# Two-layer hybrid trunk, one core: the first two projection units multiplied together, and weights loaded in half tiles

## The chip, the cores and the metric

The kernel runs on one core of a Trainium2 chip. The metric is device time of one execution in microseconds (us), the median of several runs. The engines are called as the profile calls them: PE is the matrix engine (PEld its weight loads), DVE the vector engine, ACT the scalar engine, POOL the GpSimd engine, and SP is the queue from which all DMAs of this kernel are issued.

## The reference

A residual trunk of two layers over x (1024 tokens by 1024 features, float32). Layer 0 has a gated DeltaNet head group and a sparse attention head group whose keys are picked by an indexer; layer 1 has stick-breaking attention and the HGRN2 recurrence. Each layer is a mixer and a SwiGLU feed-forward part, each between two RMS norms:

```python
for l in range(DEPTH):
    y = rms_norm(h, norm_g[l, 0])
    y = even_mixer(...) if l % 2 == 0 else odd_mixer(...)     # p = y @ w_in, heads, @ w_out
    h = h + rms_norm(y, norm_g[l, 1])
    y = swiglu(rms_norm(h, norm_g[l, 2]), w_gate[l], w_up[l], w_down[l])
    h = h + rms_norm(y, norm_g[l, 3])
```

Layer 0's `w_in` gives, among others, the 1536 columns q, k, v of the DeltaNet heads and a small group of columns for the indexer's key and the gates.

## The kernel before

**Tiling.** Features lie on the 128 partitions, tokens in two halves of 512 columns. All weights are cut into units of 128 x 1024 values (512 KB), for one feature-major unit the eight 128 x 128 blocks of one 128-column slice of a matrix. `wload` (L228) fetches a unit by one DMA into `wraw` (two buffers) and cuts it into a rounded part and a rest: ACT copies each half of 512 columns to `whi` in a rounded format (`split`, L193), and DVE for the first half, POOL for the second, subtract it from the raw values to give `wlo` (L197). `whi` and `wlo` have four half buffers each, so two units fit. The activations are cut the same way into `yhi` and `ylo` (`y_tile`, L332 and L336). A product is then three passes: `whi` by `yhi` and `whi` by `ylo` (the high passes) and `wlo` by `yhi` (the low pass), 24 matmuls of 512 columns for a feature-major unit (`dense_fm`, L264).

**Order within a unit.** `passes` (L240) takes the eight blocks in two parts of four: four high by high, four high by rest, the same for the other four, then the low pass in the same two parts. With several sums (`dense_tm`, L270, and `outproj`, L410) it goes over all sums in each part.

**The start.** `run` (L1279) calls `consts` (L150), which loads `gg` (norm gains and others) and `cc` (identity, a triangle and ones, 192 KB). `first_norm(0)` (L360) loads the eight 128 x 512 tiles of x for the first token half, cuts each into `yhi` and `ylo` with the norm's gain, and sums the squares (ACT L295 and L298, DVE L299); the inverse root mean square `rd` is applied only behind the matmuls (`norms`, L346, with the matmul with ones at L306, then ACT L308 and L309). `proj_even_a(0)` (L566) multiplies unit `U_KI` first; DVE scales the result with `rd` into `stage` (L579) and four small transposes at L583 take the gate columns from it. Then come the twelve units `U_QKV`, each followed by a scaled copy out of PSUM (`scaled`, L258), a causal convolution of four taps on DVE (L595 and three of L597), a sigmoid on ACT and a product on DVE (L600), and a store (L601). DeltaNet loads these again (L706), and its chunks start from there.

**What sets the order.** Each engine works through its instructions in a fixed order, and so does SP's queue of DMAs. A planner wrote this order beforehand from modelled times: at each moment the ready instruction with the highest priority goes next. What stands under `first()` has a far higher priority than the rest: loads, splits, norms and the work behind a matmul; the matmuls of `passes` do not. PSUM gives the projections three banks (`acc`), one the letter `b` and one `a`, three `w`.

**The end.** The last feed-forward product goes in two column halves (`down_halves`, L488), which load the same four units twice, and `last_residual` (L504) follows each.

Of the kernel before, what the change touches and what calls it, by code (L numbers as in the profile page):

```python
# [13 lines left out]
F32R = mybir.dt.float32r  # L14
# [8 lines left out]
P = 128  # L23
# [4 lines left out]
KD = 8  # L28
# [14 lines left out]
U_QKV, U_KI, U_QI, U_QB, U_KB, U_VB, U_Z = 0, 12, 13, 17, 21, 25, 29  # L43
# [68 lines left out]
class Trunk:  # L112
# [37 lines left out]
    def consts(self):  # L150
        nc, cp = self.nc, self.cp
        nc.scalar.preload_act_table_set("natural_log_exp_and_others")
        self.cc = self.t(cp, [P, C_COLS], "cc")
        c = lambda o: self.cc[:, o:o + P]
        self.ident, self.ut, self.ones = c(C_ID), c(C_U), c(C_ONES)
        self.gg = self.t(cp, [P, G_COLS], "gg")
        with self.first():
            nc.sync.dma_start(self.gg, self.ins["p_cols"])
            nc.sync.dma_start(self.cc, self.ins["c_main"])
        self.k = self.t(self.np_, [P, 8], "kk")  # L160
        nc.vector.memset(self.k[:, 0:1], -0.5)
        nc.vector.memset(self.k[:, 1:2], 1e-6)
        nc.vector.memset(self.k[:, 2:3], -0.5 * math.log(P))
        nc.vector.memset(self.k[:, 3:4], 1.0)
        nc.vector.memset(self.k[:, 4:5], 0.0)
        self.nhalf = self.k[:, 0:1]
        self.eps, self.lnscale, self.one = self.k[:, 1:2], self.k[:, 2:3], self.k[:, 3:4]
# [60 lines left out]
    def wload(self, u):  # L228
        nc = self.nc
        with self.first():  # L230
            raw = self.t(self.wp, [P, 1024], "wraw")
            nc.sync.dma_start(raw, self.ins["w_units"][u])
            w = []
            for c, e in ((slice(0, 512), nc.vector), (slice(512, 1024), nc.gpsimd)):
                w.append(self.split(raw[:, c], *(self.t(self.wp, [P, 512], n, F32R, bufs=4) for n in ("whi", "wlo")), (e,)))
        self.pace()

        return lambda o, n=P: [t[:, o % 512:o % 512 + n] for t in w[o // 512]]

    def passes(self, sums, w, first=True, last=True):  # L240

        mm = self.nc.tensor.matmul
        order = [((0, 0), (0, 1)), ((1, 0),)] if w == 0 else [((0, 0), (1, 0)), ((0, 1),)]
        n = len(sums[0][2]) // 2
        seq = [(g, ps, l[a], r[b]) for pairs in order for part in (slice(0, n), slice(n, None))
               for a, b in pairs for g, ps, terms in sums for l, r in terms[part]]
        begun, end = set(), {g: i for i, (g, *_) in enumerate(seq)}
        for i, (g, ps, l, r) in enumerate(seq):  # L250
            mm(ps, l, r, start=first and g not in begun, stop=last and end[g] == i)  # L251
            begun.add(g)
# [11 lines left out]
    def dense_fm(self, u, y):  # L264
        w = self.wload(u)
        ps = self.acc()
        self.passes([(0, ps, [(w(k * P), y.t[k]) for k in range(KD)])], 0)
        return ps

    def dense_tm(self, u0, y):  # L270

        n = HS // 2
        for c in range(2):
            ps = [self.acc() for _ in range(2)]
            for u in range(2):
                w = self.wload(u0 + 2 * c + u)
                self.passes([(tt // 2, ps[tt // 2][:, tt % 2 * n:tt % 2 * n + n],
                              [([t[:, tt * P:(tt + 1) * P] for t in y.t[4 * u + j]], w(j * n, n))
                               for j in range(4)]) for tt in range(NT)], 1, u == 0, u == 1)
            for i in range(2):  # L280
                yield 2 * i, c * n, ps[i]
# [78 lines left out]
    def first_norm(self, half):  # L360
        with self.first():
            tiles, acc, y = [], None, Y()
            for k in range(KD):
                x = self.part()
                self.nc.sync.dma_start(x, self.ins["x"][k * P:(k + 1) * P, half * HS:(half + 1) * HS])
                if half == 0:
                    self.y_tile(y, k, x, self.ng(0, 0, k))
                else:
                    acc = self.sumsq(acc, k, x)
                tiles.append(x)  # L370
            if half:
                return self.to_y(0, 0, tiles, self.inv_rms(acc))
            self.norms(y, tiles, True)
            return y
# [191 lines left out]
    def proj_even_a(self, half, y):  # L566
        nc = self.nc
        if half == 0:
            self.hist = self.t(self.np_, [P, 12, 3], "hist")
            nc.vector.memset(self.hist, 0.0)  # L570
            self.ab = self.t(self.cp, [P, 8, 16], "ab")
            self.an = self.head_gain(self.cp, "a_norm")
        ps = self.dense_fm(U_KI, y)
        with self.first():
            s = self.t(self.hp, [P, HS], "stage", bufs=2)
            if y.r is None:
                nc.vector.tensor_copy(s[0:80], ps[0:80])
            else:
                nc.vector.tensor_tensor(out=s[0:80], in0=ps[0:80], in1=y.r[0:80], op=OP.mult)  # L579
            nc.sync.dma_start(self.kiT[half], s[0:64])  # L580
            pt = self.acc()
            for tt in range(NT):
                nc.tensor.transpose(pt[:, tt * 16:tt * 16 + 16], s[64:80, tt * P:(tt + 1) * P], self.ident[64:80, 64:80])  # L583
            nc.vector.tensor_copy(self.ab[:, half * 4:half * 4 + 4, :],
                                  pt[:, 0:64].rearrange("p (t c) -> p t c", t=4))
        for ct in range(12):
            ps = self.dense_fm(U_QKV + ct, y)
            with self.first():
                xp = self.t(self.small, [P, HS + 3], "xp")
                nc.vector.tensor_copy(xp[:, 0:3], self.hist[:, ct, :])  # L590
                self.scaled(xp[:, 3:], ps, y, dve=False)
                nc.vector.tensor_copy(self.hist[:, ct, :], xp[:, HS:])
                cw = lambda j: self.gg[:, G_CONV + ct * 4 + j:G_CONV + ct * 4 + j + 1]
                s = self.t(self.hp, [P, HS], "stage", bufs=2)
                nc.vector.tensor_scalar(s, xp[:, 0:HS], cw(0), None, op0=OP.mult)  # L595
                for j in range(1, 4):
                    nc.vector.scalar_tensor_tensor(s, xp[:, j:j + HS], cw(j), s, op0=OP.mult, op1=OP.add)  # L597
                sig = self.t(self.hp, [P, HS], "sq")
                self.sigmoid(sig, s)
                nc.vector.tensor_tensor(out=s, in0=sig, in1=s, op=OP.mult)  # L600
                nc.sync.dma_start(self.qkvT[half][ct * P:(ct + 1) * P], s)  # L601
        self.tm_store(U_Z, y, self.zs[half], gain=self.an)
# [861 lines left out]
```

## Time and profile before

| | us |
|---|---|
| median of three runs | 2910.11 |
| the three runs | 2907.5 to 2910.74 |
| the profiled execution, its own time | 2903.69 |
| its span, first to last instruction | 2901.9 |
| PE busy in it | 2818.6 (97%) |

The profile is of one execution. Its page gives busy times of the engines, the span in slices, and the costliest groups of instructions; the trace behind it can be asked for the instructions in order of time (a timeline, where neighbouring instructions of one kind are merged into one row with their count), for who waited for whom, and for busy time and granted clock in any stretch. Busy PE time counts slow matmuls as fully as fast ones.

### The profile page before, as it was taken

How to read it: one execution, taken by the hardware profiler on the slowest of the kernel's cores; microseconds unless marked ns; L12 is line 12 of the kernel's file. 1: busy time of each engine (PE TensorE's matmuls, PEld its weight loads, DVE VectorE, ACT ScalarE, POOL GpSimd, SP SyncE). 2: the span in 40 equal slices, each digit the busy share in tenths (PEclk: the TensorE clock that was granted, in tenths of full speed). 3: DMA queues.
4: the chain of work that ended last, by engine and by line, in shares of the span. 5: the costliest groups of instructions: out<-in, count | busy, mean ns of one | idle time of the engine just before them, and what ended most of it. 6: DMA issues, size and time to landing. Idle time of an engine off the chain costs nothing. (4 is left out here: it accounts for less than half of the span.)

```text
span 2901.9 us, 41648 instructions
## 1 busy us (share of the span) xinstructions
PE 2818.6 (97%) x14850; PEld 2351.2 (81%) x14850; DVE 1694.5 (58%) x3037; ACT 1574.0 (54%) x2893; POOL 1123.3 (39%) x916
## 2 busy tenths in 40 slices
PE   8999999999999998999999999999999999999997
PEld 6888888878787886978788888889778778788886
DVE  7857973675656557378665235736666544732235
ACT  5545863666657585254664335536666544543333
POOL 3323332344435342255554332325555432333332
PEclk9999999999999999999999999999999999999999
DMA  5433446243333334446333334654323323543233
GB/s 196 136 121 109 144 151 209 91 146 114 103 117 107 104 121 137 139 147 202 111 109 95 100 97 125 231 156 128 98 87 107 98 89 115 167 149 98 95 95 109
DMA packets 200975, 366.63 MB, mean 126 GB/s; under 512 B 16544, under 2 KB 104640, under 8 KB 200768
## 3 DMA queue, kind: packets, MB, share of 16 engines
q1 hardware_dynamic: 200768, 363.97, 39.6%
q8 instruction: 117, 1.92, 0.3%
q14 instruction: 90, 0.74, 0.1%
HBM read 306.23 MB, written 57.67 MB: 125 GB/s over the span
## 5 line engine op out<-in xcount | busy, mean ns | idle before, releaser
L197 POOL TENSOR_TENSOR wlo<-wraw,whi 128x512 fp32r<-128x512 f32 x422 | 589.1, 1396 | 1240.3 <-PE acc L251 497.3
L193 ACT ACTIVATE whi<-wraw 128x512 fp32r<-128x512 f32 x844 | 521.6, 625 | 487.0 <-PE acc L251 431.2
L197 DVE TENSOR_TENSOR wlo<-wraw,whi 128x512 fp32r<-128x512 f32 x422 | 337.9, 801 | 470.7 <-PE acc L251 355.5
L251 PE MATMUL acc<-yhi,whi 128*128 128x512 f32 x2064 | 585.3, 400 | 11.8 <-ACT whi L193 8.0
L251 PE MATMUL acc<-ylo,whi 128*128 128x512 f32 x2064 | 581.9, 398 | 2.2 <-DVE ylo L336 2.2
L251 PE MATMUL acc<-yhi,wlo 128*128 128x512 f32 x2064 | 536.1, 396 | 0.0
L251 PE MATMUL acc<-act,whi 128*128 128x512 f32 (+1 forms) x1984 | 510.6, 393 | 21.3 <-DVE stage L452 5.7
L251 PEld LDWEIGHTS acc<-yhi,whi 128*128 128x128 f32 x2064 | 386.1, 189 | 99.5 <-ACT whi L193 8.0
L251 PEld LDWEIGHTS acc<-ylo,whi 128*128 128x128 f32 x2064 | 386.3, 189 | 88.3 <-issue 6.0
L251 PEld LDWEIGHTS acc<-yhi,wlo 128*128 128x128 f32 x2064 | 383.7, 188 | 84.1 <-issue 6.1
L251 PEld LDWEIGHTS acc<-act,whi 128*128 128x128 f32 x1984 | 363.1, 189 | 109.3 <-issue 11.5
L251 PE MATMUL acc<-act,wlo 128*128 128x512 f32 (+1 forms) x992 | 266.6, 386 | 1.4 <-POOL wlo L197 1.4
L251 PEld LDWEIGHTS acc<-act,wlo 128*128 128x128 f32 x992 | 182.0, 188 | 38.5 <-POOL wlo L197 1.8
L950 ACT ACTIVATE pen<-sc,tk 128x384 bf16<-128x384 f32 (+4 forms) x155 | 155.3, 1002 | 52.2 <-DVE tk L954 46.1
L480 DVE TENSOR_TENSOR part<-acc,part 128x512 f32<-128x512 f32 x152 | 103.8, 685 | 66.2 <-PE acc L251 66.0
L193 ACT ACTIVATE act<-stage 128x512 fp32r<-128x512 f32 x104 | 65.2, 629 | 136.9 <-DVE stage L459 117.0
L197 POOL TENSOR_TENSOR act<-stage,act 128x512 fp32r<-128x512 f32 x88 | 120.2, 1366 | 43.1 <-ACT act L193 41.0
L299 DVE TENSOR_TENSOR ssq<-ssq,sq 128x512 f32<-128x512 f32 (+1 forms) x119 | 98.7, 830 | 27.2 <-ACT sq L298 25.0
L951 DVE TENSOR_SCALAR tk<-tk 128x1 uint32<-128x1 f32 x186 | 39.3, 211 | 125.4 <-ACT pen L950 124.9
L452 DVE TENSOR_TENSOR stage<-acc,stage 128x512 f32<-128x512 f32 x66 | 45.5, 689 | 98.3 <-ACT stage L220 98.2
L251 PE MATMUL acc<-whi,yhi 128*128 128x256 f32 x640 | 100.1, 287 | 1.6 <-DVE stage L552 1.6
L251 PE MATMUL acc<-whi,ylo 128*128 128x256 f32 x640 | 101.3, 287 | 0.0
(461 smaller groups left out, 4038.1 us busy)
## 6 DMA issues: line engine op xcount, KB each, us to landing
wraw<-in_w_units_dram SPq DMA_DIRECT2D x422, 512.0 KB, 3.6
h<-part SPq DMA_DIRECT2D x40, 256.0 KB, 3.9
hld<-h SPq DMA_DIRECT2D x40, 256.0 KB, 4.6
qkvT<-stage SPq DMA_DIRECT2D x24, 256.0 KB, 2.5
kT<-kbT SPq DMA_DIRECT2D x24, 256.0 KB, 3.6
vv<-vb SPq DMA_DIRECT2D x24, 256.0 KB, 3.0
qkv<-qkvT SPq DMA_DIRECT2D x18, 256.0 KB, 3.6
part<-in_x_dram SPq DMA_DIRECT2D x16, 256.0 KB, 6.3
```

Source lines behind the costliest of these rows:

```text
L193: nc.scalar.activation(hi, src, AF.Copy)
L197: e.tensor_tensor(out=lo[:, c], in0=src[:, c], in1=hi[:, c].bitcast(F32), op=OP.subtract)
L251: mm(ps, l, r, start=first and g not in begun, stop=last and end[g] == i)
L299: nc.vector.tensor_tensor(out=acc, in0=acc, in1=sq, op=OP.add)
L452: nc.vector.tensor_tensor(out=s, in0=pg, in1=s, op=OP.mult)
L480: nc.vector.tensor_tensor(out=parts[d], in0=ps, in1=parts[d], op=OP.add)
L950: sc.activation(pen, s, AF.Sign, scale=sg, bias=nb, accum_out=n)
L951: v.tensor_scalar(rej.bitcast(U32), n, th, float(1 << b), op0=OP.is_lt, op1=OP.mult)
```

## The change

Four things change. The first two units of layer 0 (`U_KI` and the first of `U_QKV`), for the first token half only, are loaded together and go through one call of `passes` with eight steps: for each tile k of x the high passes of both units, and after all eight tiles the low pass of one unit and then of the other. Each raw unit comes by two DMAs of 256 KB into four half buffers (the same memory as before), and each half is split from its own buffer. The low pass of `passes` now goes through all the terms of one sum before the next sum, everywhere. The load of `cc` is issued in `first_norm(0)` behind the loads of x.

```diff
@@ consts
         with self.first():
             nc.sync.dma_start(self.gg, self.ins["p_cols"])
-            nc.sync.dma_start(self.cc, self.ins["c_main"])
@@ wload
         with self.first():
-            raw = self.t(self.wp, [P, 1024], "wraw")
-            nc.sync.dma_start(raw, self.ins["w_units"][u])
             w = []
             for c, e in ((slice(0, 512), nc.vector), (slice(512, 1024), nc.gpsimd)):
-                w.append(self.split(raw[:, c], *(self.t(self.wp, [P, 512], n, F32R, bufs=4) for n in ("whi", "wlo")), (e,)))
+                raw = self.t(self.wp, [P, 512], "wraw", bufs=4)
+                nc.sync.dma_start(raw, self.ins["w_units"][u][:, c])
+                w.append(self.split(raw, *(self.t(self.wp, [P, 512], n, F32R, bufs=4) for n in ("whi", "wlo")), (e,)))
         self.pace()
@@ passes
-    def passes(self, sums, w, first=True, last=True):
+    def passes(self, sums, w, first=True, last=True, steps=2):
         mm = self.nc.tensor.matmul
         order = [((0, 0), (0, 1)), ((1, 0),)] if w == 0 else [((0, 0), (1, 0)), ((0, 1),)]
-        n = len(sums[0][2]) // 2
-        seq = [(g, ps, l[a], r[b]) for pairs in order for part in (slice(0, n), slice(n, None))
-               for a, b in pairs for g, ps, terms in sums for l, r in terms[part]]
+        n = len(sums[0][2]) // steps
+        parts = [slice(i * n, (i + 1) * n) for i in range(steps)]
+        high, low = order
+        seq = [(g, ps, l[a], r[b]) for part in parts for a, b in high for g, ps, terms in sums for l, r in terms[part]]
+        seq += [(g, ps, l[a], r[b]) for a, b in low for g, ps, terms in sums for l, r in terms]
@@ behind dense_fm
+    def dense_pair(self, us, y):
+
+        ws, pss = [self.wload(u) for u in us], [self.acc() for _ in us]
+        self.passes([(i, ps, [(w(k * P), y.t[k]) for k in range(KD)]) for i, (w, ps) in enumerate(zip(ws, pss))], 0, steps=KD)
+        return pss
@@ first_norm
                 tiles.append(x)
+            if half == 0:
+                self.nc.sync.dma_start(self.cc, self.ins["c_main"])
@@ proj_even_a
-        ps = self.dense_fm(U_KI, y)
+        ps, first = self.dense_pair((U_KI, U_QKV), y) if half == 0 else (self.dense_fm(U_KI, y), None)
...
         for ct in range(12):
-            ps = self.dense_fm(U_QKV + ct, y)
+            ps = first if half + ct == 0 else self.dense_fm(U_QKV + ct, y)
```

## Rows read from the trace of the kernel before

**Rows 1.** Page, part 1: busy us, share of the span, instructions of each engine.

```profile
PE 2818.6 (97%) x14850; PEld 2351.2 (81%) x14850; DVE 1694.5 (58%) x3037; ACT 1574.0 (54%) x2893; POOL 1123.3 (39%) x916
```

**Rows 2.** Timeline of PE, 0 to 36: start, us, what, [idle before <-releaser].

```profile
8.04 0.80 PE L251 MATMUL acc<-yhi,whi 128*128 128x512 f32 x1 [8.04 <-ACT whi L193]
9.18 0.80 PE L251 MATMUL acc<-yhi,whi 128*128 128x512 f32 x1 [0.34 <-ACT yhi L332]
...
17.19 2.00 PE L251 MATMUL acc<-yhi,wlo 128*128 128x512 f32 x8
20.34 1.13 PE L306 MATMUL b<-ssq,cc 128*128 128x512 f32 x2 [1.15 <-DVE ssq L299]
...
24.57 0.42 PE L583 MATMUL acc<-cc,stage 16*128 16x16 f32 x4
24.91 1.84 PE L251 MATMUL acc<-yhi,whi 128*128 128x512 f32 x4
...
31.25 0.91 PE L858 MATMUL w<-lg,pt 32*128 32x384 f32 x2
...
33.34 1.09 PE L251 MATMUL acc<-yhi,whi 128*128 128x512 f32 x4
```

**Rows 3.** Timeline of ACT, 0 to 36.

```profile
4.51 0.72 ACT L332 ACTIVATE yhi<-part,gg 128x512 fp32r<-128x512 f32 x1 [1.68 <-DMA part<-in_x_dram]
...
7.36 1.15 ACT L193 ACTIVATE whi<-wraw 128x512 fp32r<-128x512 f32 x2 [1.62 <-DMA wraw<-in_w_units_dram]
...
14.17 0.71 ACT L332 ACTIVATE yhi<-part,gg 128x512 fp32r<-128x512 f32 x1
...
15.31 1.13 ACT L193 ACTIVATE whi<-wraw 128x512 fp32r<-128x512 f32 x2
```

**Rows 4.** Timeline of SP's queue, 0 to 45: start and length of each issue.

```profile
1.19 0.42 SPq L159 DMA_DIRECT2D cc<-in_c_main_dram  x1
1.66 0.42 SPq L365 DMA_DIRECT2D part<-in_x_dram  x1
2.12 0.43 SPq L232 DMA_DIRECT2D wraw<-in_w_units_dram  x1
2.60 3.64 SPq L365 DMA_DIRECT2D part<-in_x_dram  x7
7.36 0.33 SPq L232 DMA_DIRECT2D wraw<-in_w_units_dram  x1
```

**Rows 5.** Windows: per stretch PE, PEld, DVE, ACT, POOL busy (instructions), PEclk, DMA share, GB/s.

```profile
25.00:2901.90 2876.90, 2805.79 (x14810) 2343.67 (x14810) 1677.52 (x3003) 1557.94 (x2865) 1116.91 (x909) 0.99 0.40 125
...
19.19:24.57 5.38, 2.95 (x14) 1.56 (x13) 4.87 (x7) 1.32 (x2) 2.22 (x2) 1.00 0.89 283
26.00:27.00 1.00, 1.00 (x4) 0.71 (x4) 0.43 (x3) 0.72 (x3) 0.21 (x1) 0.50 0.20 71
```

**Rows 6.** Timeline of PE, 33 to 130: two neighbouring units in the steady stretch.

```profile
47.51 1.07 PE L251 MATMUL acc<-yhi,whi 128*128 128x512 f32 x4
...
52.95 1.07 PE L251 MATMUL acc<-yhi,whi 128*128 128x512 f32 x4
```

**Rows 7.** Timeline of DVE: the scaled copies of the units, and the idle time before.

```profile
31.42 0.69 DVE L197 TENSOR_TENSOR wlo<-wraw,whi 128x512 fp32r<-128x512 f32 x1 [3.56 <-PE acc L251]
...
33.55 0.69 DVE L258 SCALAR_TENSOR_TENSOR xp<-acc,rd 128x512 f32<-128x512 f32 x1
...
61.28 0.68 DVE L258 SCALAR_TENSOR_TENSOR xp<-acc,rd 128x512 f32<-128x512 f32 x1
...
90.59 0.68 DVE L258 SCALAR_TENSOR_TENSOR xp<-acc,rd 128x512 f32<-128x512 f32 x1
```

**Rows 8.** DMA issues by line: count, KB each, median us to landing.

```profile
wraw<-in_w_units_dram SPq DMA_DIRECT2D x422, 512.0 KB, 3.6
```

**Rows 9.** What SP's queue waited for: us in total, times, longest.

```profile
SPq L232 <- DVE wlo L197: 1131.0, 318, 10.0
```

**Rows 10.** What PE waited for, whole span: us in total, times, longest.

```profile
PE acc L251 <- POOL wlo L197: 1.4, 1, 1.4
```

## The prediction

> **What bounds the kernel now.** I read the page's busy times first: PE is busy for 97% of the span and no other engine for more than 58% [rows 1], so time is gained only where PE stands still or runs slowly: span less busy time is 2901.9 - 2818.6 = 83 us. Next I read PE's timeline at the start, because every part of the change that is not spread over the whole run acts there. Three things are to be seen in it. PE does nothing for 8.04 us, until ACT has made the first `whi` [rows 2]. From there to 17.19 it does unit KI's sixteen high matmuls one tile of x at a time, 9.18 less 8.04 = 1.1 us apart at first, because ACT hands out the tiles: ACT runs without a pause from 7.36 until the last tile at 14.17 [rows 3]. Then PE does the eight low matmuls to 19.2, waits for the sum of squares at 20.34, and has only the norm's matmuls, a bias table and four small transposes at 24.57 before unit QKV0 starts at 24.91 [rows 2]. Although QKV0's `whi` was made at 15.31 to 16.4 [rows 3], its matmuls stand behind those transposes in PE's order. The windows show it: 2.95 us of work in the 5.38 us from 19.19 to 24.57, and then a granted clock of 0.50 (the 1.2 GHz level) at 26 with PE fully busy [rows 5]. A unit in the steady stretch takes 52.95 - 47.51 = 5.44 us [rows 6]. QKV0 took from 24.91 to 33.34, 8.43 us, of which the bias table's two matmuls are 0.91 [rows 2] and two small ones that overlap them about 0.3, so about 1.8 us of it is the low clock.
>
> **The pair.** The second unit's 24 matmuls leave the path behind the transposes if they fit ahead of them. Work to fit: 24 at the steady pitch of 5.44 / 24 = 0.227 us, or 5.4 us. Room: PE stands still for 0.34 us ahead of a tile (so for three tiles), and behind the low pass 5.38 - 2.95 = 2.4 us are free [rows 2, 5]; a PE that starts earlier, with twice the work for each tile, also loses less to the slow first matmuls, whose records take 0.80 [rows 2]. So the pair's passes end near 20 to 22 and still ahead of 24.57. QKV1 then starts where QKV0 did, and one warm unit is gained: **5.4 us**. If QKV0's weights come late, its high passes fall behind tile 7 and fill only the later hole: 2.4 us at least. That is the lower bound; I take 5.4, because `whi` of QKV0 is ready at 16.4 even in the old order and the 32 matmuls left then (7.3 us) end at 23.7.
>
> **The clock.** QKV1 restarts at the low level if PE is as empty before it as QKV0 found it, and loses the 1.8 us again; with the hole filled to 20 or 22 it may not. Bounds 0 and 1.8 us gained; I take **0.8**, just under the middle, since the norm's chain of ACT and DVE still leaves a gap before 24.57. The Trainium skill, page "TensorE: Matmul & The Clock Gate", section "Why this matters for your kernels", advises against idle gaps of some microseconds between bursts of matmuls, since the clock falls back. The trace agrees at one place, 0.50 behind the half-empty stretch 19 to 24.6 [rows 5]; by the page alone the whole 1.8 would be gained if the gap closes.
>
> **The start.** `cc` leaves SP's queue ahead of x: x0 is issued at 1.19 in place of 1.66 [rows 4], 0.47 us earlier. The first weights are 256 KB in place of 512 KB. Before, x0 was used 4.51 - 1.66 = 2.85 us behind its issue, and the unit 7.36 - 2.12 = 5.24 us behind its own [rows 3, 4]. The half, issued second in the queue, should be usable between these two, at 1.66 + 2.85 = 4.5 (late enough for ACT's first two instructions) and 6.9; I take 5.3, so ACT loses its 1.62 us of idle time and PE starts at about 6 in place of 8.04. But PE's start is not the gain: ACT paces the tiles, and the pair's two further `whi` copies (1.13 us [rows 3]) may now stand ahead of tile 7. Tile 7 and with it the norm's sum and the transposes move by 0.47 + 1.62 = 2.1 us at most, by 2.1 - 1.1 = 1.0 if the copies come first, and by nothing if DVE, which adds up the squares, does not follow. I take **1.0**, bounds 0 and 2.1. `cc` is needed by the norm's matmul at 20.34 only; behind x7 it still has over 10 us, so moving it costs nothing; x1 to x7 move up by its place in the queue.
>
> **Half tiles behind the start.** 422 DMAs become 844 [rows 8]. One issue takes about 0.33 us of SP's queue [rows 4], 140 us more in 2900, on a queue that stood at this line for 1131 us waiting for DVE's splits [rows 9]: time it has. Each half now waits for its own split only, so the first half goes out earlier by DVE's lead over POOL; the second goes when the whole did. Queued behind a waiting half are the same stores and loads as behind the whole. PE waits for `wlo` from POOL once, 1.4 us, in the whole run [rows 10], so a faster arrival behind the start gives nothing: 0, with -1 to +1. At the end of the run the same four units are loaded again and ACT does wait for raw weights there; the gain is at most the lead of one half, and I take 0.3 (0 to 1.2). The Trainium skill, page "Perfetto Trace Analysis", section "DMA Optimizations", speaks on both sides: larger DMAs use the memory better, and splitting lets some work start sooner if the DMA engines are idle. The rows show no limit there: a unit of 512 KB lands 3.6 us behind its issue [rows 8], within the 5.44 us that PE takes for one [rows 6]. By the first half of that rule each unit would land later; the sum would change only through rival four.
>
> **Low pass by sums.** In `outproj` and `dense_tm` POOL's half of `wlo` is now needed after 2 low matmuls of a sum in place of 4 or 8, that is up to 6 x 0.12 = 0.7 us earlier (half-width matmuls at half of 0.227), and the first bank is finished earlier. Only where POOL is late does it cost: 1.4 us once [rows 10]. I take a loss of 0.3 (a gain of 0.5 to a loss of 3).
>
> **The sum.** 5.4 + 0.8 + 1.0 + 0.3 - 0.3 = **7.2 us** off the start, bounds by the ends: 2.4 + 0 + 0 - 1 - 3 = a loss of 1.6, and 5.4 + 1.8 + 2.1 + 1.0 + 1.2 + 0.5 = 12.0. Made against the profiled execution's 2903.69 (1.8 above its span) that gives 2896.5. That execution was 6.4 us under the median of the runs, so the median should go from 2910.1 to **2903**.
>
> **The rivals.** (1) *DVE takes the bound over, and most of the gain is given back.* In the QKV stretch DVE makes a unit every (90.59 - 61.28) / 5 = 5.86 us against PE's 5.44 [rows 6, 7], and DeltaNet starts from DVE's last product. Three `acc` banks let PE run only so far ahead. For it: the pitch. Against it: DVE stands still 3.56 us before 31.42 waiting for PE, and takes QKV0's copy at 33.55 only because the matmuls end at 33.5 [rows 2, 7]; with QKV0 finished by 22 that copy can follow `rd` at once, some 9 us earlier. If the planner leaves DVE's order as it is, about 1 to 3 us remain: 2908.
>
> (2) *It does not do what it says.* If QKV0's halves stand behind x7 in the queue, as that unit did at 7.36 [rows 4], the units do not run side by side; QKV0 only fills the hole at 19 to 24. Gain 2.4 to 5: 2906.
>
> (3) *The planner deals the rest anew.* All orders are written from modelled times, and twice the loads change them all. Behind the first 25 us PE stands still for 2876.9 - 2805.8 = 71 us [rows 5], spread over waits at changes of stage; a shift of a twentieth to a tenth of them is 4 to 7 us either way. It widens every case and has no direction of its own.
>
> (4) *Slower.* The queue of SP is in order, and each unit now holds it twice; a load needed at once (DeltaNet's chunks, the residual's tiles) then stands behind one more issue, 0.33 us [rows 4], or behind POOL's split. It decides if this falls on PE's path at more than about 20 of the changes of stage (20 x 0.33 = 7, the gain); at 40 places it is 13 us, net 6 slower: 2916. Against it: the queue's slack [rows 9].
>
> **How the numbers follow.** Forecast as summed, 0.50; rival 1, 0.22; rival 2, 0.13; rival 4, 0.15, with rival 3 spread within each. The forecast's own range is 2898 to 2906. For 8 in 10 the range must take in rivals 1 and 2 and the sum's best end: 2910.1 - 12.0 = 2898, less 2 for rival 3, is 2896; at the top, rival 1's 2908 plus 4 for rival 3 is 2912, which is also 2910.1 with the worst sum's loss of 1.6. A measurement here tells 0.2% (5.8 us, so 2904.3 and 2915.9) from no change. Faster by more: 0.42 of the forecast's 0.50 and 0.08 of rivals 1 and 2, 0.50. Slower by more: 0.10 of rival 4 and 0.01 of others, 0.11. Within: 0.39.
>
> **What would show it.** Right: PE's first matmul near 6; matmuls of both units alternating tile by tile up to about 15; QKV1's first matmul at 25 to 27 in place of 33.34; granted clock above 0.50 there; DVE's scaled copy of QKV0 before 26. Rival 1: QKV1 early, but PE waiting for `acc` or for DVE's products near 60 to 120. Rival 2: `wraw` of the second unit issued behind x7. Rival 4: longer waits of DeltaNet's and the residual's loads in SP's queue, and more idle PE at changes of stage. The prediction is wrong if QKV1 does not start at least 4 us earlier, or if PE's idle time behind 100 us differs by more than 5 us.

## The result, and the profile after

| | before | after |
|---|---|---|
| median of the runs, us | 2908.81 (4 runs) | 2888.72 (4 runs, 2884.55 to 2891.19) |
| ratio | 1 | 0.9929, interval 0.9912 to 0.9946 |
| profiled execution, us | 2903.69 | 2889.96 |
| its span, us | 2901.9 | 2888.2 |

The change makes the kernel 20.1 us faster by the medians and 13.7 us by the profiled executions. The forecast was 7.2 us and 2903; the time lies under the range's lower end of 2896. The direction was right, the size was not, and the difference does not come from the start.

The page of after, part 1 (busy us, share, instructions), answers to [rows 1]; PE's work is the same and the gain is time in which PE stood still:

```profile
PE 2819.6 (98%) x14850; PEld 2352.7 (81%) x14850; DVE 1674.9 (58%) x3037; ACT 1580.7 (55%) x2893; POOL 1117.3 (39%) x916
```

The start: PE's timeline of after, 0 to 36 us, answers to [rows 2]:

```profile
5.95 0.79 PE L252 MATMUL acc<-yhi,whi 128*128 128x512 f32 x1 [5.95 <-ACT whi L192]
...
18.37 3.83 PE L252 MATMUL acc<-yhi,wlo 128*128 128x512 f32 x16
22.04 1.02 PE L313 MATMUL b<-ssq,cc 128*128 128x512 f32 x2
23.84 1.05 PE L324 MATMUL b<-cc,ssq 128*128 128x1 f32 x8 [0.78 <-ACT rd L315]
25.22 0.42 PE L592 MATMUL acc<-cc,stage 16*128 16x16 f32 x4 [0.33 <-DVE stage L588]
25.57 1.20 PE L252 MATMUL acc<-yhi,whi 128*128 128x512 f32 x4
26.60 1.77 PE L252 MATMUL acc<-ylo,whi 128*128 128x512 f32 x4
...
33.82 1.07 PE L252 MATMUL acc<-yhi,whi 128*128 128x512 f32 x4
```

The low pass of both units (x16) ends at 22.2, and the unit that starts at 25.57 is now QKV1. SP's queue of after answers to [rows 4]; the second unit's halves go out ahead of x2 to x7:

```profile
1.19 0.42 SPq L372 DMA_DIRECT2D part<-in_x_dram  x1
1.66 0.42 SPq L233 DMA_DIRECT2D wraw<-in_w_units_dram  x1
2.13 0.43 SPq L372 DMA_DIRECT2D part<-in_x_dram  x1
2.60 1.38 SPq L233 DMA_DIRECT2D wraw<-in_w_units_dram  x3
4.02 3.50 SPq L372 DMA_DIRECT2D part<-in_x_dram  x6
7.96 0.33 SPq L379 DMA_DIRECT2D cc<-in_c_main_dram  x1
```

Now the whole run by stretch, the windows view of before (columns as in [rows 5]):

```profile
0.00:25.00 25.00, 12.79 (x41) 7.55 (x41) 16.95 (x34) 16.08 (x29) 6.37 (x7) 1.00 0.87 310
...
100.00:1080.00 980.00, 959.50 (x5371) 813.89 (x5370) 629.80 (x1432) 624.80 (x1205) 378.23 (x294) 0.99 0.40 126
1080.00:1200.00 120.00, 106.90 (x591) 87.84 (x590) 76.54 (x137) 53.19 (x95) 26.98 (x20) 0.94 0.40 128
1200.00:2300.00 1100.00, 1087.03 (x5939) 909.76 (x5939) 642.39 (x931) 572.84 (x1042) 496.26 (x433) 1.00 0.40 128
2300.00:2560.00 260.00, 253.88 (x1089) 203.01 (x1088) 145.91 (x198) 133.14 (x228) 87.57 (x66) 0.99 0.42 133
```

The same of after:

```profile
0.00:25.00 25.00, 17.67 (x58) 11.40 (x58) 17.69 (x32) 17.28 (x30) 5.86 (x8) 1.00 0.90 317
...
100.00:1080.00 980.00, 959.53 (x5362) 813.50 (x5361) 623.24 (x1434) 625.46 (x1204) 374.70 (x293) 0.99 0.41 126
1080.00:1200.00 120.00, 110.62 (x624) 91.65 (x623) 70.45 (x133) 51.89 (x91) 25.80 (x20) 0.94 0.42 130
1200.00:2300.00 1100.00, 1087.12 (x5905) 908.73 (x5904) 634.22 (x928) 578.05 (x1046) 498.07 (x435) 1.00 0.40 127
2300.00:2560.00 260.00, 259.44 (x1124) 208.86 (x1123) 146.82 (x198) 135.90 (x232) 88.95 (x67) 1.00 0.43 137
```

The length of a stretch less PE's busy time is its idle time. It falls by 17.67 - 12.79 = 4.9 us at the start, by 110.62 - 106.90 = 3.7 in 1080 to 1200 (where DeltaNet's matmuls L739 to L779 stand with little projection work beside them) and by 259.44 - 253.88 = 5.6 in 2300 to 2560, and stays within 0.1 us in the two long stretches between. So about two thirds of the idle time that is gone stood in two places far from the start, where the prediction had put nothing.

The place in 2300 to 2560 can be read in the timeline. Before, at a norm near 2480 us:

```profile
2481.16 1.02 PE L306 MATMUL b<-ssq,cc 128*128 128x512 f32 x2
...
2485.30 0.63 ACT L193 ACTIVATE whi<-wraw 128x512 fp32r<-128x512 f32 x1 [1.96 <-DMA wraw<-in_w_units_dram]
...
2485.84 0.67 ACT L308 ACTIVATE rs<-b,kk 128x512 f32<-128x512 f32 x1
...
2487.21 7.46 DVE L342 SCALAR_TENSOR_TENSOR tail<-tail,gg,rs 128x512 f32<-128x512 f32 x8 [4.53 <-ACT rs L309]
...
2495.93 2.06 PE L251 MATMUL acc<-act,whi 128*128 128x512 f32 x5 [3.50 <-DVE stage L452]
```

and after:

```profile
2473.79 1.02 PE L313 MATMUL b<-ssq,cc 128*128 128x512 f32 x2
...
2475.91 0.67 ACT L315 ACTIVATE rs<-b,kk 128x512 f32<-128x512 f32 x1
...
2477.28 6.43 DVE L349 SCALAR_TENSOR_TENSOR tail<-tail,gg,rs 128x512 f32<-128x512 f32 x8 [1.94 <-ACT rs L316]
...
2487.47 3.25 PE L252 MATMUL acc<-act,whi 128*128 128x512 f32 x12 [0.18 <-DVE stage L468]
```

Before, ACT stands for 1.96 us at a raw unit that has not landed, and behind it in ACT's order stands the norm's `rs`. It comes 4.7 us behind the start of its matmul; after, 2.1 us, since no copy that waits stands ahead of it. From `rs` hang DVE's eight products, from these, in DVE's order, the product for `stage`, and from that PE: 3.50 us idle before, 0.18 after. PE never waits *for weights* here. It waits for DVE, which waits for ACT, which waited for weights.

The waits view gives the whole run's sum for ACT (us in total, times, longest). Before:

```profile
ACT whi L193 <- DMA wraw<-in_w_units_dram: 37.0, 21, 3.6
```

After:

```profile
ACT whi L192 <- DMA wraw<-in_w_units_dram: 12.1, 11, 3.3
```

The raw load's row in part 6 of the page of after (count, KB, us from issue to landing) answers to [rows 8]; the wait of SP's queue of after answers to [rows 9]:

```profile
wraw<-in_w_units_dram SPq DMA_DIRECT2D x844, 256.0 KB, 2.7
```

```profile
SPq L233 <- DVE wlo L196: 1225.6, 362, 10.1
```

### The profile page after: what moved, and what is told of

It reads as the page before. It is cut to its first block, busy times and chain, and to the rows that moved or that the text cites. A ratio compares the mean times of both kernels' runs of the same rounds, so it can differ in the third digit from the quotient of the medians.

```text
span 2888.2 us, 42444 instructions
## 1 busy us (share of the span) xinstructions
PE 2819.6 (98%) x14850; PEld 2352.7 (81%) x14850; DVE 1674.9 (58%) x3037; ACT 1580.7 (55%) x2893; POOL 1117.3 (39%) x916
## 5 line engine op out<-in xcount | busy, mean ns | idle before, releaser
L196 DVE TENSOR_TENSOR wlo<-wraw,whi 128x512 fp32r<-128x512 f32 x422 | 346.2, 821 | 426.5 <-PE acc L252 334.7
L306 DVE TENSOR_TENSOR ssq<-ssq,sq 128x512 f32<-128x512 f32 (+1 forms) x119 | 97.2, 817 | 18.7 <-ACT sq L305 15.8
L252 PE MATMUL acc<-whi,yhi 128*128 128x256 f32 x640 | 98.8, 287 | 1.4 <-DVE stage L561 1.0
```

Of the source, the lines that this page charges most:

```text
L196: e.tensor_tensor(out=lo[:, c], in0=src[:, c], in1=hi[:, c].bitcast(F32), op=OP.subtract)
L306: nc.vector.tensor_tensor(out=acc, in0=acc, in1=sq, op=OP.add)
```

## The experiments

In the table, PE's idle time is worked out from the trace (all of it up to the last matmul, then of the first 25 us, and of two stretches that begin and end at the same weight unit in every kernel, marked by POOL's split of it: A is units 138 to 150 counted from 0, 1080 to 1200 us of before; B is units 320 to 360, 2318 to 2560). "Clock" is (1 - granted clock) times the time up to the last matmul, from the trace's clock records: the time lost where the clock fell to its 1.2 GHz level. Ratios are to the kernel before in the same session, whose median was 2907.8 to 2910.6.

| kernel | median (runs) | ratio, interval | idle | first 25 | A | B | clock | ACT for raw |
|---|---|---|---|---|---|---|---|---|
| before | 2908.81 (4) | 1 | 72.7 | 12.2 | 13.1 | 6.1 | 17.1 | 37.0 |
| b1_again: before again | 2910.89 (11) | 1.0005, 0.9996 to 1.0014 | 72.6 | 12.2 | 14.0 | 5.7 | 25.6 | 49.2 |
| p1_swap: `cc` ahead of `gg` | 2908.28 (11) | 0.9995, 0.9986 to 1.0005 | 68.1 | 11.1 | 13.8 | 5.7 | 20.5 | 36.6 |
| e4_cc: `cc` behind x | 2902.43 (11) | 0.9976, 0.9967 to 0.9984 | 68.0 | 10.2 | 13.5 | 6.0 | 20.5 | 37.7 |
| e2_pair: the pair | 2901.61 (5) | 0.9969, 0.9956 to 0.9981 | 69.1 | 9.5 | 13.9 | 6.5 | 17.1 | 39.6 |
| e3_lowpass: the low pass | 2899.43 (6) | 0.9967, 0.9955 to 0.9979 | 63.5 | 12.8 | 6.0 | 5.2 | 20.9 | 37.4 |
| e1_halves: the half tiles | 2884.84 (4) | 0.9913, 0.9900 to 0.9927 | 57.5 | 11.0 | 12.6 | 2.0 | 13.7 | 10.0 |
| h1_twodma: two DMAs, one buffer | 2896.65 (5) | 0.9962, 0.9950 to 0.9974 | 64.2 | 12.6 | 4.4 | 2.7 | 17.1 | 31.9 |
| the change | 2888.72 (4) | 0.9929, 0.9912 to 0.9946 | 57.7 | 7.3 | 9.7 | 0.6 | 18.9 | 12.1 |
| a_again: the change again | 2891.30 (5) | 0.9940, 0.9928 to 0.9952 | 60.4 | 7.4 | 9.8 | 0.8 | 17.8 | 13.4 |
| e5_whole: without half tiles | 2892.55 (5) | 0.9941, 0.9929 to 0.9954 | 60.0 | 8.6 | 5.9 | 5.1 | 14.3 | 46.8 |
| e6_nopair: without the pair | 2884.56 (4) | 0.9912, 0.9899 to 0.9926 | 55.7 | 9.9 | 9.1 | 0.6 | 10.7 | 11.5 |
| e6_again: the same again | 2888.36 (5) | 0.9933, 0.9921 to 0.9945 | 61.4 | 10.8 | 9.5 | 0.5 | 15.8 | 10.5 |
| c1_halvescc: half tiles and `cc` | 2882.86 (6) | 0.9918, 0.9905 to 0.9932 | 53.5 | 9.9 | 12.0 | 2.0 | 16.5 | 13.2 |
| c1_again: the same again | 2881.63 (4) | 0.9906, 0.9889 to 0.9922 | 49.5 | 9.6 | 10.7 | 2.0 | 17.3 | 4.3 |
| e7_oldlow: without the new low pass | 2880.98 (4) | 0.9901, 0.9887 to 0.9916 | 54.3 | 7.5 | 12.4 | 2.0 | 11.9 | 11.3 |

Idle time, clock and waits are those of one profiled execution. The granted clock is on record for every execution, to three digits, so a mean over many tells what the clock costs a kernel (some 5 us of it behind the last matmul): 28 us in before (55 executions), 22 in the change (9 with its repeat), 19 in e1_halves (4).

### Each part alone

**The half tiles alone (e1_halves).**

```diff
-            raw = self.t(self.wp, [P, 1024], "wraw")
-            nc.sync.dma_start(raw, self.ins["w_units"][u])
...
+                raw = self.t(self.wp, [P, 512], "wraw", bufs=4)
+                nc.sync.dma_start(raw, self.ins["w_units"][u][:, c])
```

> The kernel before with half tiles of raw weights alone; no pair, old low pass, constants in front. Theory S (the start carries the gain): 0 to -2 us, since the units at the start do not run together. Theory H (half tiles carry what the start does not): -8 to -15 us, with ACT's waits for raw weights falling from 37 us to about 12, PE's first matmul near 6.5, and the 3.5 us wait of PE for the product ahead of the last residual gone. Theory P (the planner's new order carries it, of either sign): a change between -6 and +6 that need not go with ACT's waits.

Measured: 2884.84, 25.7 us under before in its session, more than the whole change brought and more than the 8 to 15 of theory H. PE's idle time falls by 15.2 us, of which only 1.2 lie in the first 25 us; the other 10 or so are clock, 19 us on the mean in place of 28. ACT's wait for raw units falls from 37.0 to 10.0 us:

```profile
ACT whi L193 <- DMA wraw<-in_w_units_dram: 10.0, 11, 2.8
```

That sum does not measure what a wait costs: two executions of one kernel differ in it by 12.2 us (before, 37.0 and 49.2) or 8.9 (c1, 13.2 and 4.3), and in PE's idle time by 0.1 and 4.0. It matters where the waits stand. The term that the prediction had put at nothing is the largest of all. In B, `rs` stands ahead of the waiting copies here too, and DVE's eight products wait less:

```profile
2469.30 1.02 PE L306 MATMUL b<-ssq,cc 128*128 128x512 f32 x2
...
2472.42 0.67 ACT L308 ACTIVATE rs<-b,kk 128x512 f32<-128x512 f32 x1
...
2473.80 6.42 DVE L342 SCALAR_TENSOR_TENSOR tail<-tail,gg,rs 128x512 f32<-128x512 f32 x8 [1.94 <-ACT rs L309]
```

**The pair alone (e2_pair).** Raw units whole, `cc` in its old place, and the low pass in two parts as before.

```diff
+    def passes(self, sums, w, first=True, last=True, steps=2):
...
+        m = len(sums[0][2]) // 2
+        seq += [(g, ps, l[a], r[b]) for part in (slice(0, m), slice(m, None)) for a, b in low for g, ps, terms in sums
+                for l, r in terms[part]]
...
+        ps, first = self.dense_pair((U_KI, U_QKV), y) if half == 0 else (self.dense_fm(U_KI, y), None)
```

> The kernel before with the two first units multiplied together, from whole raw tiles, old low pass, constants in front. The orders behind the start stay nearly as before. Theory S: -12 to -20 us. Theories H and P: -4 to -6 us, one unit of 5.4 less what a later second unit loses, and PE's waits behind 100 us as before, about 60 us.

Measured: 2901.61, 8.9 us under before, the interval from 5.5 to 12.8 us (4 to 6 had been expected). Behind the start the order of PE is nearly that of before (274 of its 14850 matmuls stand elsewhere, by tiles and shapes), so this shows the start nearly alone: idle time of the first 25 us 9.5 in place of 12.2, and A and B nearly as they were. The clock loss of its profile is that of the first profile of before, 17.1; idle time falls by 3.6 us in all, and no profile shows where the rest of the 8.9 comes from. Weight unit 30 is reached at 225 us in place of 229. B keeps the same wait in its place:

```profile
2483.30 7.47 DVE L352 SCALAR_TENSOR_TENSOR tail<-tail,gg,rs 128x512 f32<-128x512 f32 x8 [5.17 <-ACT rs L319]
...
2492.03 2.00 PE L255 MATMUL acc<-act,whi 128*128 128x512 f32 x5 [4.12 <-DVE stage L462]
```

**The new low pass alone (e3_lowpass).**

```diff
+        seq += [(g, ps, l[a], r[b]) for a, b in low for g, ps, terms in sums for l, r in terms]
```

> The kernel before with the new order of the low pass alone. Theories S and H: 0 (-1 to +1), since no load changes and the start is as before. Theory P: the orders of all engines are dealt anew in about a tenth of PE's places, and the time moves by 3 to 8 us one way or the other, first where layer 0's sparse attention ends (about 230 us) or later.

Measured: 2899.43, 11 us under before, more than the 3 to 8 of theory P. The start is as before (12.8) and B nearly (5.2); A falls from 13.1 to 6.0 us. In A of before stands the longest wait of the run behind the start, DeltaNet's `dec` on DVE:

```profile
1106.81 1.11 PE L744 MATMUL a<-cc,qkv 128*128 128x128 f32 x4 [6.95 <-DVE dec L740]
```

It is there, at 6.0 to 7.0 us, in every kernel that keeps the old low pass and loads a whole unit by one DMA, and it is gone here. In the change, too, another wait is the longest of A:

```profile
1097.35 1.16 PE L1044 MATMUL w<-vv,pt 128*128 128x128 f32 x8 [2.97 <-ACT pt L1040]
```

DVE's `dec` does not use weights, and 5095 of PE's 14850 matmuls stand elsewhere than before: that points to the planner's new order and not to an earlier `wlo`, though the two were not tried apart.

**`cc` behind x alone (e4_cc), and the same load moved the other way (p1_swap).** In p1_swap it is issued ahead of `gg`.

```diff
-            nc.sync.dma_start(self.cc, self.ins["c_main"])
...
+            if half == 0:
+                self.nc.sync.dma_start(self.cc, self.ins["c_main"])
```

> The kernel before with the load of the constants behind the first tiles of x alone. All theories: -0.5 us (0 to -1), the 0.47 us by which x is issued earlier; the first matmul still waits for a whole raw unit, at about 7.5.

> The kernel before with the loads of the gains and of the constants in the other order, so that x, the weights and every order behind 40 us are as before. If moving the constants itself gave the 8 us of that run: 0 here (-2 to +1). If the executions of the kernel before carry a cost that any small shift of the first microseconds removes: -5 to -8, as there.

Measured: e4_cc 2902.43, 8.1 us under before (interval 4.7 to 9.6); p1_swap 2908.28, no difference that can be told. 0.5 us had been expected of e4_cc, nothing of p1_swap. e4_cc's first 25 us have 2.0 us less idle time, more than the 0.47 of its place in the queue, and around 1200 to 1300 us it has 2.8 less. p1_swap's profile has as little idle time (68.1), and its median is not lower. The recorded clocks part the two: the mean loss is 24 us in e4_cc and 28 in p1_swap (11 executions each), as in before. So about half of e4_cc's gain is clock; why the clock falls less in it is not shown.

### The same kernels again

**Before once more (b1_again).** No edit.

> The kernel before, unchanged, as a run of its own: ratio 1.000 within 0.1%, about 2910, and a second profile of it, to see in which stretch one execution of it differs from another (the profile shown of it took 2903.7, its median is 2910).

Measured: 2910.89, ratio 1.0005. The two profiles of before have the same idle time, 72.7 and 72.6, and spans of 2901.9 and 2910.4. The clock losses, 17.1 and 25.6, hold all of these 8.5 us. A profile that is 6 us under the median, as that of before is, was one in which the clock fell less.

**The change once more (a_again), and without the pair (e6_nopair, e6_again).**

```diff
-        ps, first = self.dense_pair((U_KI, U_QKV), y) if half == 0 else (self.dense_fm(U_KI, y), None)
+        ps, first = self.dense_fm(U_KI, y), None
...
-            ps = first if half + ct == 0 else self.dense_fm(U_QKV + ct, y)
+            ps = self.dense_fm(U_QKV + ct, y)
```

> The changed kernel without the pair. If the pair's 5 us at the start are kept to the end: about 5 us above the changed kernel, 2893 to 2895. If they are lost or covered behind the start once half tiles are there (half tiles alone took 2884.8): as the changed kernel or faster, 2884 to 2889.

> The changed kernel again, beside the one without the pair on the same chip: 2887 to 2891, ratio 0.993.

> The changed kernel without the pair again. If the pair costs behind the start what it gains there or more: 2882 to 2887, below the changed kernel run beside it. If the first comparison was chance of the clock: within 1 us of the changed kernel or above it.

Measured: without the pair 2884.56 and 2888.36, with it 2888.72 and 2891.30. a_again lies just above its range, e6_again between its two expectations. In the one session that held both kernels, 2888.36 stands against 2891.30, with intervals that overlap. So the pair brings nothing beside the other three parts, and may cost 3 us; its 2.5 to 3.5 us less idle time in the first 25 us is there each time, and given back later.

### What the half tiles do

**The change with whole raw units (e5_whole).**

```diff
-                raw = self.t(self.wp, [P, 512], "wraw", bufs=4)
-                nc.sync.dma_start(raw, self.ins["w_units"][u][:, c])
...
+            raw = self.t(self.wp, [P, 1024], "wraw")
+            nc.sync.dma_start(raw, self.ins["w_units"][u])
```

> The changed kernel with whole raw units again (pair, new low pass and constants behind x kept). Theory H: much of the gain goes, 2897 to 2903, with ACT's waits for raw weights back near 37 us. Theory P: the time is one more draw of the planner, 2885 to 2905, with no regard to ACT's waits; the start alone (pair) keeps 5 us of gain.

Measured: 2892.55, against 2888.72 and 2891.30 with half tiles: 1 to 4 us, not the 25.7 that they bring alone (theory H had 2897 to 2903). Part is hidden by the clock, which takes 22 us from the change on the mean and 18.5 from this kernel (5 executions). What is sure of the half tiles returns: ACT's wait for raw units is 46.8 again and B is 5.1. But A is 5.9 in place of 9.7, since with the new low pass the order differs there.

**Two DMAs of half a unit into one whole buffer (h1_twodma).** Each half lands nearly as early as in the change; the buffer comes free only when both halves are split.

```diff
-            nc.sync.dma_start(raw, self.ins["w_units"][u])
+            for c in (slice(0, 512), slice(512, 1024)):
+                nc.sync.dma_start(raw[:, c], self.ins["w_units"][u][:, c])
```

> The kernel before with each raw unit loaded by two DMAs of 256 KB into the one whole buffer, so that a half can be split when it has landed, but no load starts before both splits of the unit two back are done. If the earlier landing of a half is what helps (whole units hold ACT in front of a norm): 2888 to 2896, ACT's waits for raw weights 12 to 25 us, and PE's idle time from unit 320 to 360 (about 2318 to 2560 us) down from 6 us to under 2. If the buffer that comes free in halves is what helps: 2904 to 2911, waits over 30 us, that idle time still about 6 us.

Measured: 2896.65, 11 us under before, just above what was expected if the landing is what helps. A half lands 2.9 us behind its issue, but ACT still waits 31.9 us in all:

```profile
ACT whi L193 <- DMA wraw<-in_w_units_dram: 31.9, 23, 3.1
```

So the earlier landing by itself takes little of ACT's waits away; with the earlier release of the buffer, in e1_halves, over two thirds of them go. B is 2.7, much nearer to that of the half tiles, so at that place the landing did most. But most of this kernel's own gain in idle time is in A, 4.4 in place of 13.1, where e1_halves gains next to nothing (12.6): a matter of the order, which differs from before in 4330 of 14850 matmuls here and in 5617 in e1_halves. So how the gain of e1_halves divides between landing, release and order is not settled. More raw buffers of whole units, which would give the release without the landing, were not tried.

### Which parts to keep

**Half tiles and `cc` alone (c1_halvescc, c1_again), and with the pair (e7_oldlow).** c1 is e1_halves with e4_cc's edit. e7_oldlow is the change with the old low pass:

```diff
-        seq += [(g, ps, l[a], r[b]) for a, b in low for g, ps, terms in sums for l, r in terms]
+        m = len(sums[0][2]) // 2
+        seq += [(g, ps, l[a], r[b]) for part in (slice(0, m), slice(m, None)) for a, b in low for g, ps, terms in sums
+                for l, r in terms[part]]
```

> Half tiles and the constants behind x, but no pair and the old low pass. If the gains of the start add to half tiles alone (2884.8): PE starts near 5.7 and the time is 2879 to 2883. If the time goes by the planner's order of the low pass: as half tiles alone, 2883 to 2887, or worse.

> The change with the low pass taken back to two parts for all sums (the pair, the half tiles and the moved load of the constants stay); that is c1_halvescc with the pair added. Theory (the pair brings forward only the start, by 3 to 5 us, and the rest is the half tiles'): 2878 to 2880, idle time of PE in the first 25 us 7 to 8, that of the units 320 to 360 (2300 to 2550 us) at most 2, below c1_halvescc by 3 to 5 us. Rival (what the pair brings is paid back at the next changes of stage, as the whole change against itself without the pair suggests): 2883 to 2889, first 25 us 7 to 8 as well, idle time behind 100 us 3 to 6 us more than in c1_halvescc. Second rival (the new low pass is what costs beside half tiles, not the pair): at or below c1_halvescc and 6 us or more below the whole change's 2889 to 2891.

> The kernel before with the half tiles and the moved load of the constants alone, once more, beside e7_oldlow. If its lead over the whole change was real: 2880 to 2886, PE's idle time 52 to 56 us. If it was the spread between sessions: 2887 to 2892.

Measured: c1 2882.86 and 2881.63, e7_oldlow 2880.98, the last two in one session. The lead of c1 over the change was real. e7_oldlow lies between the two first expectations: the pair adds 0.7 us, which can't be told from nothing. c1_again's idle time, 49.5 us, is below the 52 to 56 that was expected; behind 100 us e7_oldlow has 4.6 us more, as its rival said, and a clock loss of 11.9 for 17.3 makes up for that. The pair does bring the start forward: POOL's split of weight unit 4 comes at 33 us in place of 38, and PE reaches DeltaNet's first product at 98.8 in place of 102.8. Then the lead goes in three places that c1_again does not have: a granted clock of 0.92 from 100 to 120 us (1.6 us), a wait of 1.74 us for DVE's `stage` at 506, and one of 0.99 for ACT's `lg` at 729. From about 780 us the two run level.

The second rival of that expectation holds where the pair is there too: beside half tiles the new low pass costs. e7_oldlow is 7.7 us under the change's first runs and 10.3 under its second, though in other sessions; its ratio's interval ends at 0.9916 and those of the change begin at 0.9912 and 0.9928. Without the pair it is less sure: c1_halvescc is 5.5 us under e6_again in one session, with intervals that overlap, and in their other runs, of different sessions, the two lie 3 us apart. Two places show it. One is around 920 us, where PE now waits 4.7 us for `dec` of another DeltaNet chunk, in all four runs that have both half tiles and the new low pass; behind it the granted clock falls too, another 1.7 to 3.4 us. In the change:

```profile
914.95 2.44 PE L252 MATMUL acc<-act,whi 128*128 128x512 f32 x10
922.09 1.12 PE L753 MATMUL a<-cc,qkv 128*128 128x128 f32 x4 [4.71 <-DVE dec L749]
```

The windows of 910 to 940 us, of the change and of e7_oldlow:

```profile
910.00:940.00 30.00, 25.29 (x114) 20.79 (x113) 26.20 (x37) 10.84 (x19) 13.22 (x11) 0.89 0.24 76
```

```profile
910.00:940.00 30.00, 30.00 (x148) 25.09 (x147) 23.63 (x44) 15.07 (x27) 14.45 (x11) 1.00 0.32 98
```

4.7 us idle and 0.11 x 30 = 3.3 us of clock are 8 us. In e7_oldlow, projection work is still there to fill the wait. The other is 1290 to 1540 us, with 6.9 us idle in the change and 1.9 in e7_oldlow; A gives 2.7 back. The new low pass costs at 920 us without half tiles as well: from weight unit 118 to 126, e3_lowpass and e5_whole stand idle 4.5 and 4.2 us, against 2.9 in the five runs with whole units and the old low pass, and 0.0 to 0.2 in the four with half tiles and the old one. h1_twodma, with the old low pass, has 5.5 there. By the medians c1 and e7_oldlow are the fastest of all, 25 to 30 us under before and 6 to 10 us under the change; by the ratios (0.9901 to 0.9918) they can't be told from e1_halves (0.9913) or e6_nopair (0.9912). So, as far as these runs tell, the half tiles alone would have done.

**The parts do not add.** Alone they bring 25.7, 11.1, 8.9 and 8.1 us, 54 in all; together 20. The half tiles and the low pass each give all engines a new order, and the order of both together is a third one, with waits of its own. In A the new low pass takes 7 to 8 us of idle time away with whole units and 1 to 3 with half tiles; around 920 us it adds 1.4 to 1.6 with whole units and 4.5 to 4.7 with half tiles.

## Why the prediction was wrong

**The start: right in kind, 2 us too high.** The pair, the clock and the start were put at 5.4 + 0.8 + 1.0 = 7.2 us. By the profile they are 5.0: before, QKV1 began at 33.34 [rows 2]; after, QKV2 begins at 33.82, one unit of 5.44 us further on [rows 6] but 0.48 later. PE's first matmul is at 5.95 (forecast: near 6). QKV1 begins at 25.57 (forecast: 25 to 27), and the pair's work ends at 22.2 (20 to 22). Two terms fell. *The start's 1.0* is a loss of 0.65: the transposes came at 25.22 and not 24.57, since the norm's matmul L313 now stands behind sixteen low matmuls and begins at 22.04, not 20.34. The prediction had filled PE's hole and not asked what stands behind the filling. *The clock's 0.8* was 0.2 in the change: QKV1 takes 33.82 - 25.57 = 8.25 us, QKV0 took 8.43. In the other kernels with the pair (e2_pair, e5_whole, e7_oldlow) the granted clock there is 1.00, so the term lay within its range. These are the windows of 26 to 30 us of before, of the change and of e7_oldlow:

```profile
26.00:30.00 4.00, 4.00 (x13) 3.14 (x13) 0.92 (x4) 1.77 (x6) 1.04 (x1) 0.67 0.38 116
```

```profile
26.00:30.00 4.00, 4.00 (x13) 3.12 (x12) 3.43 (x15) 2.27 (x8) 0.88 (x1) 0.59 0.34 94
```

```profile
26.00:30.00 4.00, 4.00 (x18) 3.31 (x19) 3.97 (x17) 2.67 (x9) 0.58 (x1) 1.00 0.40 130
```

**Half tiles behind the start: the step that failed.** The term was put at 0, with 1 us either way, because "PE waits for `wlo` from POOL once, 1.4 us, in the whole run" [rows 10]. The row is right and the conclusion is not: only PE's direct waits for weights were looked at. The row that mattered was ACT's, 37.0 us at raw units, with the whole of ACT's order behind each wait. What the runs show as the half tiles' own, in whatever order: B falls from 5.1 to 6.5 us in the seven runs with whole raw loads to 0.5 to 2.0 in the eight with half tiles; the stretch of 1550 to 2080 us falls from 1.4 to 1.9 to 0.4 to 0.7; and 1.7 to 3.4 us of clock loss inside B, in all seven, is there in only one of the eight (1.7). That is some 6 to 11 us, and B's part of it can be followed wait by wait, as above. The other 15 to 20 of the 25.7 of e1_halves are waits and clock loss that also go or stay with the order; they are not divided further, and their cause stays open.

The prediction saw no limit in the loads because the old landing lay within a unit's 5.44 us. That is a comparison with PE's pace; the one who waited was ACT. A half lands 2.7 us behind its issue in place of 3.6. The Trainium skill, "Perfetto Trace Analysis", "DMA Optimizations", says that splitting DMAs into smaller ones may let some work start sooner; the traces agree, but h1_twodma shows that this is only part of what the half tiles bring.

**The planner's new deal (rival 3): mis-sized.** It was put at 4 to 7 us in either direction. New orders in these runs moved the time by 11 us (e3_lowpass, by A alone 7), and by 8 to 10 us between the change and e7_oldlow. That it has no direction is not shown: alone, each of the single parts gained; between the change and e7_oldlow a new order lost. Of the 71 us of idle time that it was measured against, 10.6 lie behind the last matmul and are no waits at changes of stage.

**The low pass: wrong sign and size.** A loss of 0.3 was taken, with -3 to +0.5. Alone it gains 11 us, beside the other parts it costs 8 to 10, and neither by POOL's lateness, on which its bounds rested: PE waits for POOL's `wlo` 1.4 us in before, 0 in e3_lowpass and 0.8 in the change. What is left is the order, though that was not tried by itself.

**The end: right.** 0.3 was taken, with 0 to 1.2. From weight unit 360 on PE's idle time falls from 6.9 to 6.1 us, and the time behind the last matmul grows from 10.6 to 11.0: 0.5 gained.

**The reference point.** The sum was made against the profiled 2903.69 and then lifted by 6.4 us to the median. That profile had 8.5 us less clock loss than the repeat of before; the change's profile stands 1.2 us *above* its median. So 13.7 us in the profiles are 20.1 in the medians, and part of the miss against 2903 is this: against the profiled execution the forecast was 2896.5 and the change's was 2889.96. By the recorded clocks about 6 of the 20 us are clock (28 us in before, 22 in the change), of which the forecast had only the 0.8 at the start.

**The other rivals.** DVE's pace (1) did not take the start's gain in the change: PE's units keep their 5.44 us in the QKV stretch, DeltaNet's first product comes at 98.7 us in place of 105.2, and weight unit 33 is reached at 252.1 in place of 257.3. The second unit behind x7 (2) is refuted by SP's rows above. The queue of SP (4) waits longer for DVE's splits, 1225.6 us for 1131.0 [rows 9], and PE's idle time has grown in none of the windows above. The forecast's own sign of error, PE's idle time behind 100 us moving by over 5 us, is what happened: 59.6 to 49.4.

## What to carry to other kernels

A load may be worth far more than the bottleneck engine's own wait for it: look, for each engine that works in a fixed order, at what it waits for in the whole run, and at what stands behind the wait. Test each part of a change alone and also take each out of the whole: here one of the four brought more than all four together, and one that gained 11 us alone cost 8 to 10 beside the others. Where a planner writes the order of everything, no edit is local, and a range drawn from the edited stretch is too narrow; here its lower end was 7 us too high.

## What the runs showed of the hardware

Span less PE's idle time, less the 10.6 to 11.3 us behind the last matmul, less the clock loss, is 2800.6 to 2802.7 us in all sixteen profiles, whatever the edit; so a time here is full-speed work plus idle time plus clock loss. The clock takes 11 to 26 us of a run, a fifth to a third of what idle time takes, and differs by 8.5 us between two profiles of the same program with the same idle time (72.7 and 72.6). It is not fixed by the idle time just before: in the change and in e7_oldlow PE stands idle for the same 0.78 and 0.33 us around the norm's matmuls ahead of QKV1, and the granted clock behind it is 0.59 in one and 1.00 in the other. The Trainium skill, "TensorE: Matmul & The Clock Gate", "Why this matters for your kernels", advises against idle gaps between bursts of matmuls. No run here shows that closing these decides the level: e5_whole has 1.37 us of idle time there and a granted clock of 1.00.
